# First loads of an encoder trunk on two queues, in smaller parts, and the first tile scaled ahead of the squares

## The chip, the cores and the metric

The kernel runs on one core of a Trainium2 chip. The metric is the device time of one execution, in microseconds (us). PE is the matmul engine, DVE and ACT are the vector and the scalar engine, POOL is GpSimd, and SP is the engine that issues most of the transfers; "SPq" and "ACTq" in the trace are transfers being issued on the queue of SP and of ACT.

## The reference

Two layers over 256 tokens of width 1024. Cut to what matters:

```python
for l in range(DEPTH):                       # DEPTH = 2
    h = rmsnorm(x, norm_g[l])
    proj = h @ w_in[l]                       # 1024 x 5120
    xa, za, qb, kb, vb, zb, qc, kc, vc, zc = jnp.split(proj, split_points, axis=-1)
    ya = ssm_branch(xa, ...) * jax.nn.silu(za)        # bidirectional state space group
    yb = na_branch(qb, kb, vb, na_rpb[l]) * jax.nn.silu(zb)
    yc = dilated_branch(qc, kc, vc, t5_bias) * jax.nn.silu(zc)
    x = x + jnp.concatenate([ya, yb, yc], axis=-1) @ w_out[l]
return rmsnorm(x, final_g)
```

The change lies in what comes first: x and the first weights are loaded, the squares of x give the RMS factor, and `h @ w_in[0]` begins.

## The kernel before, in words

All activations lie transposed: 128 partitions, 8 blocks k of the model width, 256 tokens. A layer multiplies h by w_in in 20 jobs c of 256 columns. A job has two weight pieces (k 0 to 3 and k 4 to 7), each `[4, 256]` per partition, 512 KB, in a buffer `raw`. Six jobs of layer 0 (0, 1, 2, 3, 5 and 8) are plain: PE reads the fp32 weights from `raw`. For the others ACT or DVE make a high part (`whi`) and DVE a low part (`wlo`), and PE does three matmuls for one. After the 20 jobs, among which the state space group and the heads are worked off, come the jobs of the output projection (`mix0`, `mix1`, `mix2`).

Jobs 0 and 1 of layer 0 don't wait for the RMS factor: they read `gx`, which is x times the gain `ng` (`scaled`, L1358: one 128x256 tile per k, on ACT or DVE), and the factor `rstd` is multiplied in afterwards, where DVE makes `xa`. From job 2 on PE reads `xin`, x with gain and `rstd` (`normed`, L1370, on DVE), and its split `h0h`, `h0l`, `h1h`, `h1l` (`split_h`, L1387). The way to `rstd`: ACT squares two k at a time (`sqx`), DVE adds the squares, PE sums over partitions (`psn<-ones,sqx`), ACT takes a root and DVE refines it (`nr`), PE spreads it (`psn<-ident,nr`), ACT copies it. In the same stretch DVE and ACT also make the state space group's tables (`sva`, `svb`, `lbar`, `pw`, `pt`, `q1`, `tmi`, `wt`); PE transposes `wt` in groups of four matmuls (`psw<-ident,wt`).

In the first microseconds `read_x` (L1528) issues on SP the gain, and then in turn a part of x (two k, 256 KB) and half of a weight piece (256 KB). The ACT queue carries one load only, the state space parameters `lam`. `load_pieces` (L474) follows on SP with the other pieces.

The order of the work on every engine is fixed when the program is built. Each piece of work is a generator that yields the engine it wants next and the events it waits for; a planner (`Flow`) keeps a clock for every engine from its own cost formulas, and emits what can start first, ranked by the tables `RANK` and `PATIENCE`. `in_order` then ties each engine to that order. Where the planner sees PE with nothing to do it puts in filler matmuls (`warm`, L438, called at L320 to L326), whose results nobody reads. All other instructions go through one helper and have line L135 in the trace, so tiles and not lines tell them apart.

Of the kernel before, what the change touches and what calls it, by code (L numbers as in the profile page):

```python
# [340 lines left out]
def trunk(ctx: ExitStack, tc: tile.TileContext, io):  # L341
# [18 lines left out]
    def dma(out, src):  # L360
        SP.dma_start(out, src)
# [25 lines left out]
    def events(n):  # L387
        return [Event() for _ in range(n)]
# [75 lines left out]
    class Piece:  # L464


        def __init__(self, src, plain=False):
            self.src, self.plain, self.by_dma = src, plain, False
            self.half_ev, self.raw_ev, self.hi_ev, self.ev = Event(), Event(), Event(), Event()

        def free(self):
            flow.free(*(("raw",) if self.plain else ("whi", "wlo")))
# [1 line left out]
    def load_pieces(pieces):  # L474
        for w in pieces:
            yield "SP", "raw"
            w.raw = new("raw", [4, 256])
            dma(w.raw, w.src)
            flow.set(w.half_ev)
            flow.set(w.raw_ev)  # L480
            if w.plain:
                flow.set(w.ev)
# [926 lines left out]
    def run_layer(L):  # L1409
# [3 lines left out]
        for kind, c, kgs in L.jobs:  # L1413
            if kind == "in":
# [4 lines left out]
                for kh in range(2):  # L1419
                    w = next(it)  # L1420
                    for kk in range(4):
                        yield "PE", w.half_ev if w.plain and kk < 2 else w.ev, (L.g_ev if early else L.h_ev if w.plain else L.hs_ev)[4 * kh + kk]
                        hx, h = (L.gx if early else L.hx)[kh], L.h[kh]
                        for ct in range(2):
                            first, last = kh == 0 and kk == 0 and ct == 0, kh == 1 and kk == 3
                            o = ps[:, ct * 256:(ct + 1) * 256]
                            cs = slice(ct * P, (ct + 1) * P)
                            if w.plain:
                                a, b = w.raw[:, kk, cs], hx[:, kk, :]
                                if toks:  # L1430
                                    a, b = hx[:, kk, cs], w.raw[:, kk, :]
                                mm(o, a, b, first, last)
                            elif toks:
                                mm3(o, [t[:, kk, cs] for t in h], [w.hi[:, kk, :], w.lo[:, kk, :]], first, last)
                            else:
                                mm3(o, [w.hi[:, kk, cs], w.lo[:, kk, cs]], [t[:, kk, :] for t in h], first, last)
                    w.free()
# [87 lines left out]
    LAST_PLAIN = [max(n, default=0) for n in PLAIN]  # L1525
    L0 = layers[0]

    def read_x():  # L1528

        yield "SP", "qkv", "qkv"  # L1530
        L0.hx = [new("qkv", [4, S], name=f"xin{i}") for i in range(2)]
        load_gain(L0)
        for i in range(4):
            dma(L0.hx[i // 2][:, 2 * (i % 2):2 * (i % 2) + 2, :], io["x"][:, 2 * i:2 * i + 2, :])
            flow.set(xin_ev[i])
            flow.cur.pend = 0.0

            w, k = pieces[i // 2], 2 * (i % 2)
            if k == 0:
                yield "SP", "raw"  # L1540
                w.raw = new("raw", [4, 256])
            else:
                yield "SP"
            dma(w.raw[:, k:k + 2, :], w.src[:, k:k + 2, :])
            flow.set(w.half_ev if k == 0 else w.raw_ev)
            if k:
                flow.set(w.ev)
            flow.cur.pend = 0.0
            yield "SP"
        flow.spawn(place_gx(L0))  # L1550
        yield "A", "atn"
        sq = new("atn", [8, S], name="sqx")
        done = events(4)
# [6 lines left out]

    def square_x(i, sq, ev, done):
        yield "A", ev
        flow.spawn(scaled(L0, 2 * i, 2))
        s = sq[:, 2 * i:2 * i + 2, :]
        A.activation(s, L0.hx[i // 2][:, 2 * (i % 2):2 * (i % 2) + 2, :], AF.Square)
        if i > 0:
# [12 lines left out]
        for ev in n.ev:  # L1579
            flow.set(ev)  # L1580

    begin, xin_ev = Event(), events(4)
    pieces = [w for L in layers for w in L.pieces]
    begin.t = 1.2
    flow.spawn(keep_warm(WARM[0], begin, L0.hs_ev[7]))
# [101 lines left out]
```

## Time and profile before

| | us |
|---|---|
| median of 3 runs | 459.48 (458.31 to 461.18) |
| profiled execution | 457.03 |
| its span in the trace | 455.2 |
| PE busy in the span | 444.5 |
| DVE busy | 349.6 |
| ACT busy | 301.5 |

The profiled execution is the one that the trace shows; its time contains the span and about 1.8 us around it. The mean granted clock of PE in it is 0.997. A row of a timeline gives the start, the length, the engine, the line, the operation, out<-in and the count; an fp32 matmul of 256 columns by fp32 weights leaves two records, so a count of 8 is four matmuls. Times in the text are those of the span's start unless said otherwise.

### The profile page before, as it was taken

What the parts mean: (1) busy time and instruction counts of PE and PEld (TensorE: products, weight loads), DVE (VectorE), ACT (ScalarE), POOL (GpSimd) and SP (SyncE); (2) the same over time, 40 slices, a digit from 0 to 9 for tenths busy, and PEclk for the clock granted to TensorE, in tenths of its full rate; (3) what the DMA queues carried; (4) which work ended last, traced back from release to release, by engine and by line L of the source; (5) the groups of instructions that cost most, each with busy time, mean ns of one, the idle gap of its engine ahead of it and who ended that gap; (6) DMA issues with size and microseconds to landing.
All of it is one profiled execution on the core that took longest, in us unless ns stands there. A gap on an engine that the chain in (4) does not pass through costs nothing.

```text
span 455.2 us, 11299 instructions
## 1 busy us (share of the span) xinstructions
PE 444.5 (98%) x4484; PEld 412.4 (91%) x4484; DVE 349.6 (77%) x747; ACT 301.5 (66%) x607; POOL 30.6 (7%) x61
## 2 busy tenths in 40 slices
PE   8999999998999999999999999999999999999994
PEld 7779899788888999999998999998998999999994
DVE  5899979998798688879728889499899654468533
ACT  6444889784687866846534687967787793756532
POOL 1020031210000000000000110232000000000000
PEclk9999999999999999999999999999999999999998
DMA  7755362545767344545626844755564654554503
GB/s 261 247 176 194 103 193 77 146 134 161 275 186 225 123 137 144 175 159 179 212 110 199 245 146 124 195 152 167 174 192 144 204 169 130 195 182 151 177 1 93
DMA packets 46005, 75.79 MB, mean 166 GB/s; under 512 B 20944, under 2 KB 29264, under 8 KB 45952
## 3 DMA queue, kind: packets, MB, share of 16 engines
q1 hardware_dynamic: 45808, 74.97, 52.3%
q8 instruction: 35, 0.57, 0.5%
q14 instruction: 18, 0.15, 0.1%
q10 hardware_dynamic: 144, 0.10, 0.1%
HBM read 70.38 MB, written 4.67 MB: 165 GB/s over the span
## 4 chain that ended last, share of the span: by engine, by line
PE 78%; DVE 9%; DMA 6%; ACT 3%; issue 1%; SPq 1%; POOL 0%; DVEq 0%; ACTq 0%; POOLq 0%
PE pj L135 58%; PE psy L135 4%; PE po L135 3%; PE sc L135 3%; PE psx L135 3%; PE pp L135 3%; DMA xad<-xa 2%; DMA raw<-w_in 2%; PE psn L135 2%; PE psw L135 2%; DMA xin<-x 1%; DMA bias<-rpb 1%; PE psr L135 1%; DVE t1s L135 1%; DVE wlo L135 1%
## 5 line engine op out<-in xcount | busy, mean ns | idle before, releaser
L135 DVE TENSOR_TENSOR wlo<-raw,whi 128x1024 fp32r<-128x1024 f32 x92 | 113.9, 1238 | 44.7 <-PE pj L135 25.5
L135 ACT CAST whi<-raw 128x1024 fp32r<-128x1024 f32 x92 | 96.1, 1046 | 63.1 <-PE pj L135 39.8
L135 PE MATMUL pj<-h0h,whi 128*128 128x256 f32 x192 | 57.2, 298 | 0.0
L135 PE MATMUL pj<-h1h,whi 128*128 128x256 f32 x192 | 56.2, 292 | 0.0
L135 PE MATMUL pj<-h0l,whi 128*128 128x256 f32 x192 | 54.3, 283 | 0.0
L135 PE MATMUL pj<-h1h,wlo 128*128 128x256 f32 x192 | 54.2, 283 | 0.0
L135 PE MATMUL pj<-h0h,wlo 128*128 128x256 f32 x192 | 54.2, 283 | 0.0
L135 PE MATMUL pj<-h1l,whi 128*128 128x256 f32 x192 | 54.2, 282 | 0.0
L135 POOL TENSOR_TENSOR bias<-bias,namask 128x160 f32<-128x160 f32 x32 | 25.6, 802 | 214.7 <-DMA bias<-rpb 177.3
L135 PEld LDWEIGHTS pj<-h0h,whi 128*128 128x128 f32 x192 | 36.7, 191 | 2.2 <-issue 1.9
L135 PEld LDWEIGHTS pj<-h1h,whi 128*128 128x128 f32 x192 | 36.7, 191 | 1.5 <-issue 1.2
L135 PEld LDWEIGHTS pj<-h0h,wlo 128*128 128x128 f32 x192 | 36.7, 191 | 0.1
L135 PEld LDWEIGHTS pj<-h1h,wlo 128*128 128x128 f32 x192 | 36.7, 191 | 0.0
L135 PEld LDWEIGHTS pj<-h1l,whi 128*128 128x128 f32 x192 | 36.7, 191 | 0.0
L135 PEld LDWEIGHTS pj<-h0l,whi 128*128 128x128 f32 x192 | 36.6, 191 | 0.0
L135 PE MATMUL pj<-xin,raw 128*128 128x256 f32 x128 | 31.4, 385 | 0.2 <-DVE xin L135 0.2
L135 ACT ACTIVATE pt<-pt,nm 128x160 f32<-128x160 f32 (+1 forms) x64 | 29.5, 463 | 0.8 <-DVE nm L135 0.7
L135 ACT ACTIVATE pt<-pt,sm 128x256 f32<-128x256 f32 (+1 forms) x62 | 26.9, 465 | 3.6 <-DVE sm L135 3.5
L135 PEld LDWEIGHTS pj<-xin,raw 128*128 128x128 f32 x128 | 22.9, 190 | 4.4 <-DVE xin L135 1.3
L135 ACT COPY E<-psx 64x512 f32<-64x512 f32 x32 | 18.6, 580 | 7.4 <-PE psx L135 6.9
L135 ACT COPY ptt<-pp 128x512 f32<-128x512 f32 x32 | 18.7, 585 | 6.8 <-PE pp L135 6.6
L135 PE MATMUL pj<-gx,raw 128*128 128x256 f32 x96 | 22.4, 384 | 0.0
(196 smaller groups left out, 1201.7 us busy)
## 6 DMA issues: line engine op xcount, KB each, us to landing
raw<-w_in SPq DMA_DIRECT2D x78, 512.0 KB, 3.7
raw<-w_out SPq DMA_DIRECT2D x24, 512.0 KB, 3.2
bias<-vdram SPq DMA_DIRECT2D x16, 192.0 KB, 3.4
raw<-glu_w SPq DMA_DIRECT2D x4, 512.0 KB, 3.1
bias<-rpb SPq DMA_DIRECT2D x16, 120.0 KB, 3.9
xin<-x SPq DMA_DIRECT2D x4, 256.0 KB, 5.2
raw<-w_in SPq DMA_DIRECT2D x4, 256.0 KB, 4.9
cc<-c_p SPq DMA_DIRECT2D x2, 512.0 KB, 6.4
```

The costliest lines, as they stand in the source:

```text
L135: return f(*args, **kw)
```

## The change

x goes out on SP in five parts (k 0, k 1, k 2-3, k 4-5, k 6-7). The two pieces of job 0 and the gain go out on the ACT queue (`read_w`), the first piece in parts k 0, k 1 and k 2-3, the second in two halves, each part with an event of its own on which PE waits. `half_ev` goes. Tiles of `gx` are asked for one by one, the one of k 0 before the squares.

```diff
--- before.py
+++ after.py
@@ -466,7 +466,7 @@
 
         def __init__(self, src, plain=False):
             self.src, self.plain, self.by_dma = src, plain, False
-            self.half_ev, self.raw_ev, self.hi_ev, self.ev = Event(), Event(), Event(), Event()
+            self.raw_ev, self.hi_ev, self.ev, self.part_ev = Event(), Event(), Event(), None
 
         def free(self):
             flow.free(*(("raw",) if self.plain else ("whi", "wlo")))
@@ -476,7 +476,6 @@
             yield "SP", "raw"
             w.raw = new("raw", [4, 256])
             dma(w.raw, w.src)
-            flow.set(w.half_ev)
             flow.set(w.raw_ev)
             if w.plain:
                 flow.set(w.ev)
@@ -1419,7 +1418,7 @@
                 for kh in range(2):
                     w = next(it)
                     for kk in range(4):
-                        yield "PE", w.half_ev if w.plain and kk < 2 else w.ev, (L.g_ev if early else L.h_ev if w.plain else L.hs_ev)[4 * kh + kk]
+                        yield "PE", w.part_ev[kk] if w.part_ev else w.ev, (L.g_ev if early else L.h_ev if w.plain else L.hs_ev)[4 * kh + kk]
                         hx, h = (L.gx if early else L.hx)[kh], L.h[kh]
                         for ct in range(2):
                             first, last = kh == 0 and kk == 0 and ct == 0, kh == 1 and kk == 3
@@ -1525,29 +1524,38 @@
     LAST_PLAIN = [max(n, default=0) for n in PLAIN]
     L0 = layers[0]
 
+    def read_w():
+
+        L0.ng = one("ng", [KD], bufs=2)
+        for n, w in enumerate(pieces[:2]):
+            w.part_ev = events(4)
+            for k, size in ((0, 1), (1, 1), (2, 2)) if n == 0 else ((0, 2), (2, 2)):
+                if k == 0:
+                    yield "A", "raw"
+                    w.raw = new("raw", [4, 256])
+                else:
+                    yield "A"
+                A.dma_start(w.raw[:, k:k + size, :], w.src[:, k:k + size, :])
+                for i in range(k, k + size):
+                    flow.set(w.part_ev[i])
+                flow.cur.pend = 0.0
+                if n == k == 0:
+                    A.dma_start(L0.ng, io["norm_g"][0])
+                    flow.set(L0.ng_ev)
+                    flow.cur.pend = 0.0
+
     def read_x():
 
         yield "SP", "qkv", "qkv"
         L0.hx = [new("qkv", [4, S], name=f"xin{i}") for i in range(2)]
-        load_gain(L0)
-        for i in range(4):
-            dma(L0.hx[i // 2][:, 2 * (i % 2):2 * (i % 2) + 2, :], io["x"][:, 2 * i:2 * i + 2, :])
-            flow.set(xin_ev[i])
-            flow.cur.pend = 0.0
-
-            w, k = pieces[i // 2], 2 * (i % 2)
-            if k == 0:
-                yield "SP", "raw"
-                w.raw = new("raw", [4, 256])
-            else:
-                yield "SP"
-            dma(w.raw[:, k:k + 2, :], w.src[:, k:k + 2, :])
-            flow.set(w.half_ev if k == 0 else w.raw_ev)
-            if k:
-                flow.set(w.ev)
+        flow.spawn(read_w())
+        for k, size in ((0, 1), (1, 1), (2, 2), (4, 2), (6, 2)):
+            dma(L0.hx[k // 4][:, k % 4:k % 4 + size, :], io["x"][:, k:k + size, :])
+            flow.set(x0_ev if k == 0 else xin_ev[k // 2])
             flow.cur.pend = 0.0
             yield "SP"
-        flow.spawn(place_gx(L0))
+        flow.spawn(place_gx(L0, x0_ev))
+        flow.spawn(scaled(L0, 0, 1))
         yield "A", "atn"
         sq = new("atn", [8, S], name="sqx")
         done = events(4)
@@ -1560,7 +1568,8 @@
 
     def square_x(i, sq, ev, done):
         yield "A", ev
-        flow.spawn(scaled(L0, 2 * i, 2))
+        for k in range(1 if i == 0 else 2 * i, 2 * i + 2):
+            flow.spawn(scaled(L0, k, 1))
         s = sq[:, 2 * i:2 * i + 2, :]
         A.activation(s, L0.hx[i // 2][:, 2 * (i % 2):2 * (i % 2) + 2, :], AF.Square)
         if i > 0:
@@ -1579,7 +1588,7 @@
         for ev in n.ev:
             flow.set(ev)
 
-    begin, xin_ev = Event(), events(4)
+    begin, x0_ev, xin_ev = Event(), Event(), events(4)
     pieces = [w for L in layers for w in L.pieces]
     begin.t = 1.2
     flow.spawn(keep_warm(WARM[0], begin, L0.hs_ev[7]))
```

Since a planner sets the order, it moves in places that the diff does not name. In the rows below `[waits ...]` names the counters that the instruction waits for: DMAHW0 to DMAHW7 are eight counters that the transfers of all queues use in turn, so a transfer that reuses one is issued after the earlier transfer on it has landed; the other names are engines.

ACT, from its first transfer on, before (raw is a weight piece, xin0 and xin1 are x, the numbers behind names tell buffers apart):

```order
L135 DMA svb_90<-lam 128x192
L135 ACTIVATE sqx_104<-xin0_84 128x512 [waits DMAHW1_49]
L135 ACTIVATE gx0_111<-xin0_84,ng_86 128x256 [waits DMAHW0_49]
L135 ACTIVATE gx0_111<-xin0_84,ng_86 128x256
L135 ACTIVATE sqx_104<-xin0_84 128x512 [waits DMAHW4_49]
L135 ACTIVATE gx0_111<-xin0_84,ng_86 128x256 x2
L135 ACTIVATE sqx_104<-xin1_85 128x512 [waits DMAHW6_49]
L135 ACTIVATE gx1_112<-xin1_85,ng_86 128x256 x2
L135 ACTIVATE sqx_104<-xin1_85 128x512 [waits DMAHW0_49]
L135 ACTIVATE gx1_112<-xin1_85,ng_86 128x256 x2
```

And ACT after the change:

```order
L135 DMA raw_89<-w_in 128x256
L135 DMA ng_86<-norm_g 128x8
L135 DMA svb_97<-lam 128x192
L135 DMA raw_89<-w_in 128x256 [waits DMAHW0_49]
L135 DMA raw_89<-w_in 128x512 [waits DMAHW2_49]
L135 DMA raw_107<-w_in 128x512 [waits DMAHW3_49]
L135 ACTIVATE sqx_101<-xin0_84 128x512 [waits DMAHW1_49]
L135 ACTIVATE gx0_105<-xin0_84,ng_86 128x256 [waits DMAHW5_49]
L135 ACTIVATE gx0_105<-xin0_84,ng_86 128x256
L135 DMA raw_107<-w_in 128x512 [waits DMAHW6_49]
L135 ACTIVATE sqx_101<-xin0_84 128x512
L135 ACTIVATE sqx_101<-xin1_85 128x512 [waits DMAHW4_49]
```

Between the loads of `lam` and the first square there now stand three transfers that wait for a landing: that of x k 0 (DMAHW0), of x k 2-3 (DMAHW2) and of the first part of the weights (DMAHW3); a fourth, before the second square, waits for x k 6-7 (DMAHW6). The first square still stands ahead of the first `gx`; on DVE the tiles k 2 and k 3 of `gx` are now its first work after two memsets.

PE at its start, after the change (before, 12 `warm`, 12 `gx` matmuls, and then the two of `psn<-ones,sqx`):

```order
L438 MATMUL warm_95<-ident_63 128x128 [waits Pool_49]
L438 MATMUL warm_95<-ident_63 128x128 x8
L135 MATMUL pj_92<-gx0_105,raw_89 128x256 [waits DMAHW3_49,Activation_49]
L135 MATMUL pj_92<-gx0_105,raw_89 128x256
L135 MATMUL pj_92<-gx0_105,raw_89 128x256 [waits DMAHW0_49,Activation_49]
L135 MATMUL pj_92<-gx0_105,raw_89 128x256
L438 MATMUL warm_95<-ident_63 128x128 x3
L135 MATMUL pj_92<-gx0_105,raw_89 128x256 [waits DMAHW2_49,DVE_49]
L135 MATMUL pj_92<-gx0_105,raw_89 128x256
L135 MATMUL psn_164<-ones_64,sqx_101 128x1 [waits DVE_49]
L135 MATMUL psn_164<-ones_64,sqx_101 128x1
L135 MATMUL pj_92<-gx0_105,raw_89 128x256 x2
```

The `psn<-ones,sqx` pair stands behind 6 matmuls of `gx`, and no longer behind 12. There are 9 `warm` ahead of the first and 3 between, where there were 12 ahead; the four that stood between the matmuls of job 2 are gone.

PE at the end of layer 0, where the `mix0` part of an output job ends, before:

```order
L135 MATMUL pj_2649<-mix0h_2175,wlo_2614 128x256
L135 MATMUL pj_2649<-mix0l_2176,whi_2561 128x256
L438 MATMUL warm_1982<-ident_63 128x128
L135 MATMUL pj_2649<-mix1h_2643,whi_2616 128x256 [waits Activation_49]
L135 MATMUL pj_2649<-mix1h_2643,wlo_2665 128x256 [waits DVE_49]
L135 MATMUL pj_2649<-mix1l_2644,whi_2616 128x256 [waits DVE_49]
```

And after the change:

```order
L135 MATMUL pj_2587<-mix0h_2203,wlo_2539 128x256
L135 MATMUL pj_2587<-mix0l_2204,whi_2503 128x256
L438 MATMUL warm_1935<-ident_63 128x128 x10
L135 MATMUL psw_2638<-ident_63,wt_2554 128x128 [waits DVE_49,Activation_49]
L135 MATMUL psw_2638<-ident_63,wt_2554 128x128 x3
L438 MATMUL warm_1935<-ident_63 128x128 x3
L135 MATMUL psw_2652<-ident_63,wt_2554 128x128 [waits DVE_49,Activation_49]
L135 MATMUL psw_2652<-ident_63,wt_2554 128x128 x3
L438 MATMUL warm_1935<-ident_63 128x128 x7
L135 MATMUL psw_2668<-ident_63,wt_2643 128x128 [waits DVE_49,Activation_49]
L135 MATMUL psw_2668<-ident_63,wt_2643 128x128 x3
L135 MATMUL pj_2587<-mix1h_2575,whi_2537 128x256
```

Twenty `warm` stand here instead of one, around three groups of `psw` of the next layer, which before stood among earlier jobs; a second single `warm` that followed 12 matmuls later is gone. In layer 1 both programs have the same order. In jobs 3 and 4 the change has two `psw` groups ahead of the first matmul of job 4, before it has four.

## Rows read from the trace of the kernel before

**Rows 1.** Page, engines: busy us (share of the span), instructions.

```profile
PE 444.5 (98%) x4484; PEld 412.4 (91%) x4484; DVE 349.6 (77%) x747; ACT 301.5 (66%) x607; POOL 30.6 (7%) x61
```

**Rows 2.** Timeline of SP's queue, 0 to 12: start us, us, engine, instruction, count.

```profile
1.19 0.42 SPq L135 DMA_DIRECT2D xin<-x  x1
2.12 0.45 SPq L135 DMA_DIRECT2D xin<-x  x1
...
7.00 0.56 SPq L135 DMA_DIRECT2D cc<-c_p  x1
```

**Rows 3.** Chain that ended last, 0 to 33: start us, us, what.

```profile
2.12 4.86 DMA xin<-x
```

**Rows 4.** Timeline of ACT, 0 to 33; in brackets idle time before and its releaser.

```profile
0.94 0.38 ACTq L135 DMA_DIRECT2D svb<-lam  x1
...
4.41 0.63 ACT L135 ACTIVATE sqx<-xin 128x512 f32<-128x512 f32 x1 [2.18 <-DMA xin<-x]
4.95 0.89 ACT L135 ACTIVATE gx<-xin,ng 128x256 f32<-128x256 f32 x2
...
14.11 0.26 ACT L135 ACTIVATE nr<-psn,epst 128x2 f32<-128x2 f32 x1
...
16.03 0.37 ACT L135 COPY rstd<-psn 128x256 f32<-128x256 f32 x1 [1.36 <-PE psn L135]
```

**Rows 5.** Timeline of DVE, 0 to 33.

```profile
4.53 1.01 DVE L135 SCALAR_TENSOR_TENSOR sva<-sva 128x64 f32<-128x64 f32 x4
7.66 0.69 DVE L135 TENSOR_TENSOR sqx<-sqx 128x512 f32<-128x512 f32 x1 [2.13 <-ACT sqx L135]
...
11.65 0.41 DVE L135 TENSOR_TENSOR sqx<-sqx 128x256 f32<-128x256 f32 x1
```

**Rows 6.** Timeline of PE, 0 to 42.

```profile
1.36 4.89 PE L438 MATMUL warm<-ident 128*128 128x128 f32 x24 [1.36 <-POOL ident masks.py:199]
6.16 5.64 PE L135 MATMUL pj<-gx,raw 128*128 128x256 f32 x24
12.12 0.60 PE L135 MATMUL psn<-ones,sqx 128*128 128x1 f32 x4 [0.31 <-DVE sqx L135]
...
15.28 0.71 PE L135 MATMUL psn<-ident,nr 128*128 128x128 f32 x4
...
23.02 2.16 PE L135 MATMUL pj<-xin,raw 128*128 128x256 f32 x8
...
27.69 0.61 PE L438 MATMUL warm<-ident 128*128 128x128 f32 x4
28.46 4.64 PE L135 MATMUL pj<-xin,raw 128*128 128x256 f32 x20 [0.16 <-DVE xin L135]
...
33.37 1.89 PE L135 MATMUL pj<-xin,raw 128*128 128x256 f32 x8
35.10 0.60 PE L135 MATMUL psw<-ident,wt 128*128 128x128 f32 x4
...
40.55 0.47 PE L135 MATMUL pj<-h0h,whi 128*128 128x256 f32 x1
```

**Rows 7.** Windows: us, busy time of each engine, PEclk, DMA share, GB/s.

```profile
8.00:10.00 2.00, 2.00 (x10) 1.71 (x10) 1.93 (x9) 2.00 (x6) 0.00 (x0) 1.00 1.03 344
...
20.00:40.00 20.00, 19.83 (x98) 16.43 (x98) 19.83 (x51) 7.30 (x19) 3.47 (x6) 1.00 0.61 189
```

**Rows 8.** PE's waits between 33 and 204: us in total, times, longest.

```profile
PE sc L135 <- ACT k L135: 1.3, 1, 1.3
PE pp L135 <- issue: 0.5, 1, 0.5
```

**Rows 9.** Timeline of PE at the end of layer 0.

```profile
209.96 0.39 PE L438 MATMUL warm<-ident 128*128 128x128 f32 x2
...
210.31 0.28 PE L135 MATMUL pj<-mix1h,wlo 128*128 128x256 f32 x1
210.42 0.29 PE L135 MATMUL pj<-mix1l,whi 128*128 128x256 f32 x1
```

## The prediction

> **What bounds the kernel now.** First the engines' line of the page [rows 1]: PE is busy for 444.5 us, 98% of the span of 455.2, in a fixed order. So a change pays only where PE idles or does filler, and costs wherever it puts either on PE. Then PE's timeline of the start [rows 6] shows where it isn't doing useful work: 4.89 us of filler from 1.36 to 6.16, the first real matmul at 6.16, and job 2 (`pj<-xin`), which begins at 23.02 but is fed by DVE with filler between, so that its second half and job 3 run only from 28.46. A plain matmul takes 1.73 / 4 = 0.43 us (8 records from 33.37 to 35.10), so the 16 of job 2 in one run would have ended at 29.9, and not at 28.46 + 8 x 0.43 = 31.9. Job 4 begins at 40.55. Behind the front, PE waits in layer 0 for 1.3 us (`sc<-k,q`) and for 0.5 us [rows 8].
>
> The other engines there: ACT squares x for 0.63 us a part and makes two tiles of `gx` in 0.89 [rows 4]; DVE adds squares, and between them works on `sva` at 0.25 us an instruction (4 in 1.01) [rows 5]; from 20 to 40 DVE is busy for 19.83 of 20 us [rows 7]. In the chain, x k 2-3, issued at 2.12, lands at 6.98 [rows 3]. The SP queue issues `cc` at 7.00, right behind that landing [rows 2]: an issue whose counter is still in use holds its queue until the earlier transfer is in.
>
> **The change, part by part.** All sums are against the profiled execution, 457.03 us, which is 2.45 us under the median of the runs shown.
>
> *Issues.* Three transfers leave SP (two weight halves of the first piece, the gain) and two more of the second piece; six come to ACT, at 0.38 us each by the one that stands there [rows 4] or 0.42 to 0.45 as on SP [rows 2]. The first three cost nothing, since ACT waits for x anyway until 4.41. The next three stand ahead of ACT's first square, and by the order each waits for a landing: x k 0, x k 2-3 and the first weight part. So x k 2-3 must be in before two issues, 0.85 us, and only then ACT begins to compute, though the square itself needs x k 0 and k 1 only. When does x k 2-3 land? At the earliest like the first x load of before, of as many bytes, 4.4 us [rows 4]; at the latest like the same part of before, 6.98. Ahead of it and with it are now about 740 KB against 870 KB before (sum of the loads issued by then on both queues); from 2 us on, where the first loads land, (6.98 - 2) x 740 / 870 gives 6.2 us as an estimate, and since it is issued half a microsecond earlier I take 6.0.
>
> *First tile.* 6.0 + 0.85 + the square (0.54, by the spacing 4.41 to 4.95) + a tile of `gx` (0.45, half of 0.89) gives the first real matmul at 7.9 us instead of 6.16. With the early bound it is 6.3. So the first tile isn't earlier in any case.
>
> *Squares and `rstd`.* Now ACT waits for x k 6-7 with a transfer before the second square: in by 8.4 us by the same scaling (bounds 6.5 and 9.6), plus 0.45, then square, square, two `gx`, square (3 x 0.54 + 0.8) to about 11.4, then DVE's two adds (0.69 and 0.41) to 12.5: `psn` at 12.5 against 12.12 [rows 6]. By then only 6 of 16 matmuls of job 0 are done, where before 12 were, because the order puts `psn` ahead of the others. Behind the last add DVE now has 11 instructions of `sva`, 11 x 0.25 = 2.7 us, ahead of its four of `nr`, which took 0.9 from ACT's end at 14.37 [rows 4] to PE's start at 15.28 [rows 6]: `psn<-ident,nr` at about 16.1. ACT's two lookups of `svb` stand ahead of `rstd` and wait for eight more `sva`, 2 us: `rstd` at about 18, not 16.03 [rows 4].
>
> *PE to job 4.* From 12.12 to 23.02 [rows 6] before has 10.9 us for 20 plain matmuls, 8.6, and 2.3 of other work. Now from 12.5: 26 matmuls x 0.43 = 11.2, the same 2.3, and 0.5 of wait, as `psn` (0.6) and 6 matmuls reach only to about 15.6: job 1 ends at 26.5, 3.5 us after 23.02. There the change gets something back: DVE and ACT now make `xin`, `h0` and `h1` ahead of the state space tables, so `xin` is there when PE comes. Job 2 takes 6.9 us instead of 9, and job 3 6.9 plus two `psw` groups of 0.45 (0.60 [rows 6] less the overlap with their neighbours). Job 4 starts at 26.5 + 6.9 + 6.9 + 0.9 = 41.2, 0.65 after 40.55 [rows 6], with two groups, 0.9 us, still to do: **+1.55 us**. If the landings come at the early bounds, 1.9 less for the last part of x: -0.4; if at the late ones, 1.2 more: +2.8.
>
> *Tables put off.* What DVE did from 16 to 23 us for the state space group comes after 26 us. DVE is full there [rows 7], so some of its products will be late for PE in jobs 4 and 5. A `wlo` that is late by a part of its own length: **+0.4 us** (0 to 1, where its slack is used up).
>
> *Later waits in layer 0.* A later PE swallows waits whose releasers aren't later too: from 1.8 us gone to as much again added. I take a gain of less than half: **-0.7 us** (-1.8 to +2).
>
> *Filler at the end of layer 0.* The order has 18 more `warm` there. Before, from the one `warm` at 209.96 to the second matmul after it 0.35 us pass, of which a matmul takes 0.11 to 0.12 [rows 9]: 0.23 each, 0.22 in a row of them (4 records in 0.61, with the end of the last [rows 6]). **+4.0 us**. They run whether or not PE has anything to wait for, and in before PE waits there for nothing at all [rows 8]. If DVE's late `wt` makes PE wait longer than the filler, it is more.
>
> Sum: 1.55 + 0.4 - 0.7 + 4.0 = **+5.25 us**, 462.3 in terms of the profiled execution, 464.7 of the median.
>
> **Row and rule, the first loads.** The transfers are busy at 1.03 of their engines' time from 8 to 10 us, at 344 GB/s [rows 7], fed by one queue nearly alone. The Trainium skill, "DMA: Bandwidth & Descriptors", section "Issuing engines are not separate DMA queues", says that transfers started on several engines end up on the same 16 and interleave, and that only issue time is saved. By that rule a second queue moves no byte earlier; the row agrees. It speaks against the early bounds above, which are already the less likely end.
>
> **The rivals.**
> *Nothing that can be measured.* The front is even, as the recovered 2 us of job 2 balance the later start, and the later waits shrink by 1.8: +4.0 + 0.4 - 1.8 = +2.6, 462.1 of the median, +0.6%. For it: job 2's starvation is large in the rows. Against: `rstd` is bound by DVE's `sva`. 0.35.
> *Faster.* Loads land at the early bounds, so the front gives back 1.9 + the whole of job 2's stall, about -4, and the moved tables let the waits of 1.8 go too. With the filler it is -1.8, 457.7. It decides at x k 6-7: in before 7.5 us. It can pass 1% (4.6 us) only if the filler isn't paid, that is if it takes the place of waits. 0.06 for all of it, 0.04 beyond 1%.
> *Slower still.* DVE, some 4 us behind at 30 us, doesn't catch up before the first whole `wlo` are due, and PE waits 3 to 4 us more in jobs 4 to 9: 468. For it: 19.83 of 20 us busy. Against: DVE is busy for 349.6 of 455.2 us in all [rows 1]. 0.13.
> *The clock.* In before, the first fillers take 4.89 / 12 = 0.41 us each [rows 6], later ones 0.22: PE begins at half pace, 1.2 GHz, and by the matmuls after 6.16 (24 records in 5.64, with waits on ACT) it is at 2.4. Now the 9 fillers end at about 5.2, and PE does nothing until 7.9. What it does at half pace before `psn` has room; if the first four matmuls behind `psn` still go at it, they cost 4 x 0.43 = 1.7 us more: 466.4. The longest idle time of PE after the start in before is 1.3 us [rows 8], so no row shows 2.7. 0.10. The Trainium skill, "TensorE: Matmul & The Clock Gate", section "Part 1: The HAM clock gate", says that activity releases a throttle and idleness brings it back, which is this rival; no run here shows it yet.
> *The change doesn't do what it says* is already in the forecast: the built order squares first.
>
> **How the numbers follow.** The forecast has 0.36, the four rivals 0.35, 0.06, 0.13 and 0.10. Likeliest time **464.7 us**. Eight in ten: from 459 (between the even and the faster case) to 469 (both slower mechanisms in part). A measurement of this kernel can tell about 1%, 4.6 us, from no change: 464.1 is the bound. The forecast lies at it, so half of its chance and all of the two slower rivals, with a tenth for sizes that I have too small, are slower: 0.50; faster 0.05; within 0.45.
>
> **What would show it.** Right: first real matmul between 6.3 and 8.7, `psn` at about 12.5, `rstd` after 17, job 2 in one run of about 7 us, job 4 between 40 and 42.5, and `warm` of 4 us at about 212 us with no idle time beside. Wrong: an ACT that squares at 4 us (then the transfers don't hold it), job 1 ending by 24, or fillers standing where PE would have waited anyway: then the `psw` behind them still shows a wait.

## The result and the profile after

The change makes the kernel slower: 466.50 us (465.96 to 467.94, four executions) against 460.33 (458.31 to 461.5, four) beside it. The ratio is 1.0144 [1.0096, 1.0191], or +6.2 us, against a forecast of 464.7 and +5.25. The profiled execution took 465.96 us with a span of 464.1, 8.9 more than that of before; 2.8 of these 8.9 arise behind the last `mix1` job, and are told apart below. Ratios leave out executions in a slower state of the clock; experiments 1 and 3 each have one among the four executions of their median, and the profile of experiment 3 is of it.

The page's line of engines answers to [rows 1] (busy us, share of the span, instructions):

```profile
PE 452.7 (98%) x4512; PEld 421.7 (91%) x4512; DVE 350.5 (76%) x748; ACT 299.2 (64%) x605; POOL 27.3 (6%) x61
```

PE is as full as before, and has only 28 records more. So the loss isn't idle time; it is PE's own work, which takes longer or is filler. The front shows the first kind. The chain that ended last, from 1.66 (start us, us, what):

```profile
1.66 4.33 DMA xin<-x
...
6.00 0.33 ACTq L135
...
6.38 0.45 ACTq L135
...
6.88 0.63 ACT sqx L135
```

ACT's timeline, answering to [rows 4]:

```profile
3.23 3.60 ACTq L135 DMA_DIRECT2D raw<-w_in  x3
...
17.78 0.37 ACT L135 COPY rstd<-psn 128x256 f32<-128x256 f32 x1 [0.86 <-PE psn L135]
```

The square at 6.88 needs x k 0 and k 1 only, yet stands behind three issues that last from 3.23 to 6.83, because the second of them waits for x k 2-3, in at 5.98. The last releaser that the view names is this landing; the two issues behind it (0.33 and 0.45) are the rest of the price. PE's timeline, to be laid beside [rows 6]:

```profile
1.35 4.21 PE L438 MATMUL warm<-ident 128*128 128x128 f32 x18 [1.35 <-POOL ident masks.py:199]
7.96 3.78 PE L135 MATMUL pj<-gx,raw 128*128 128x256 f32 x8 [2.40 <-ACT gx L135]
11.53 1.49 PE L438 MATMUL warm<-ident 128*128 128x128 f32 x6
12.81 1.45 PE L135 MATMUL pj<-gx,raw 128*128 128x256 f32 x4
14.10 0.50 PE L135 MATMUL psn<-ones,sqx 128*128 128x1 f32 x4
14.46 2.84 PE L135 MATMUL pj<-gx,raw 128*128 128x256 f32 x12
...
27.36 9.01 PE L135 MATMUL pj<-xin,raw 128*128 128x256 f32 x41
```

After 2.40 us without work the first four matmuls take (11.53 - 7.96) / 4 = 0.89 us each, twice the 0.43 of [rows 6]; the 12 records from 14.46 are at 0.45 again. The 9 fillers ahead of the gap ran at half pace too, 0.43 us apart up to the last, so in this execution PE had not come to full pace when its work ran out. `psn` could have run when DVE's last add ended at 11.90, and came at 14.10. From 27.36 on job 2 runs without a gap, and job 3 up to a wait of 0.99 us for `wt` ahead of the `psw` at 40.60. DVE's timeline (the counterpart of [rows 5]):

```profile
6.00 0.62 DVE L135 TENSOR_SCALAR gx<-xin,ng 128x256 f32<-128x256 f32 x2 [5.11 <-DMA xin<-x]
...
11.48 0.42 DVE L135 TENSOR_TENSOR sqx<-sqx 128x256 f32<-128x256 f32 x1
...
28.84 0.29 DVE L135 TENSOR_TENSOR lbar<-svb,sva 128x128 f32<-128x128 f32 x1
```

In before `lbar` was there at 14.10:

```profile
14.10 0.29 DVE L135 TENSOR_TENSOR lbar<-svb,sva 128x128 f32<-128x128 f32 x1
```

So DVE idles for 5.11 us for x k 2-3, which its first tile of `gx` needs, with the tables' work queued behind. `lam`, which that work reads, was itself in only at about 6.2 (issued at 1.84, 4.4 us to its landing), so with another order on DVE the tables, which began at 6.54, would not have begun much earlier. The sum rows of two sets of windows, 0 to 14 and 14 to 40, say how much it lost (sum of us, then each engine's busy time). Before:

```profile
sum 14.00, PE 12.33 PEld 10.83 DVE 8.61 ACT 9.87 POOL 1.38; mean PE 2.06 PEld 1.80 DVE 1.43 ACT 1.64 POOL 0.23
sum 26.00, PE 25.83 PEld 20.83 DVE 24.89 ACT 9.99 POOL 3.47; mean PE 6.46 PEld 5.21 DVE 6.22 ACT 2.50 POOL 0.87
```

After:

```profile
sum 14.00, PE 10.25 PEld 8.99 DVE 5.88 ACT 6.07 POOL 1.38; mean PE 1.71 PEld 1.50 DVE 0.98 ACT 1.01 POOL 0.23
sum 26.00, PE 25.61 PEld 21.33 DVE 21.68 ACT 9.72 POOL 2.48; mean PE 6.40 PEld 5.33 DVE 5.42 ACT 2.43 POOL 0.62
```

By 40 us DVE has done 27.6 us of work instead of 33.5, though in all it does the same [rows 1]: 5.9 us are still to do. Of these 2.7 are lost by 14 us and 3.2 later, where DVE waits 3.6 us instead of 0.6, 1.67 of it for the transfer of `xa`. The work between doesn't make up for it: by 190 us DVE has done 154.2 us instead of 162.9. The lag shows at the end of layer 0, where DVE makes layer 1's `wt`. PE's matmuls on it before, and then after (duration in ns, first and last start in us):

```profile
L135 PE MATMUL psw<-ident,wt x32: 271/272/273, 165.0 to 185.7; 128*128 128x128 f32 x32
```

```profile
L135 PE MATMUL psw<-ident,wt x32: 270/273/273, 186.8 to 208.4; 128*128 128x128 f32 x32
```

They stand 22 us later, six of the eight groups past the start of `mix0`, and fillers stand ahead of three of them. PE's timeline after, where before has one `warm`, at 192.24 (that of [rows 9] is another one, 17.7 us later, which after has too, at 216.44):

```profile
192.01 2.40 PE L438 MATMUL warm<-ident 128*128 128x128 f32 x20
194.25 0.60 PE L135 MATMUL psw<-ident,wt 128*128 128x128 f32 x4
194.68 0.83 PE L438 MATMUL warm<-ident 128*128 128x128 f32 x6
195.35 0.60 PE L135 MATMUL psw<-ident,wt 128*128 128x128 f32 x4
195.79 1.73 PE L438 MATMUL warm<-ident 128*128 128x128 f32 x14
197.35 0.60 PE L135 MATMUL psw<-ident,wt 128*128 128x128 f32 x4
197.71 0.36 PE L135 MATMUL pj<-mix1h,whi 128*128 128x256 f32 x1
```

PE's longest waits between 33 and 204, answering to [rows 8] (us in total, times, longest):

```profile
PE psw L135 <- DVE wt L135: 1.0, 1, 1.0
PE pp L135 <- POOL bias L135: 0.7, 1, 0.7
```

The first places where each job begins give the account. A group of `psw` that is still to do counts 0.43 us (194.25 to 194.68):

| PE's first matmul of | before | after | later by | groups of `psw` still to do, more than before | lag |
|---|---|---|---|---|---|
| job 4 | 40.55 | 43.17 | 2.62 | 2 | 3.5 |
| `mix0` | 189.36 | 189.06 | -0.30 | 6 | 2.3 |
| `mix1` | 192.38 | 197.71 | 5.33 | 3 | 6.6 |
| `mix2` | 213.20 | 219.68 | 6.48 | 0 | 6.5 |
| last `mix1`, layer 1 | 436.46 | 442.55 | 6.09 | 0 | 6.1 |
| last matmul | 449.43 | 458.71 | 9.28 | 0 | 9.3 |

So 3.5 us are lost in the front, and 1.2 come back in the jobs: 0.9 of it as waits, which were 1.8 in [rows 8] and are now 0.7 and one of 0.2 (the wait for `wt` of 1.0 lies ahead of job 4). Between `mix0` and `mix1` 4.3 are added, which is 19 fillers of 0.23. From the last `mix1` to the last matmul 3.2 more are lost, and that is the clock. Windows of after (us, busy time of each engine, PEclk, DMA share, GB/s):

```profile
440.00:450.00 10.00, 10.00 (x89) 10.00 (x88) 2.84 (x4) 2.81 (x7) 0.00 (x0) 1.00 0.01 2
450.00:451.00 1.00, 1.00 (x10) 1.00 (x9) 0.00 (x0) 0.97 (x3) 0.00 (x0) 0.78 0.00 0
...
453.00:459.00 6.00, 6.00 (x29) 5.84 (x28) 2.35 (x7) 1.37 (x4) 0.00 (x0) 0.50 0.30 87
```

The granted clock falls to the 1.2 GHz level at about 450.5 with PE busy throughout, and a matmul that took 0.11 us takes 0.21. The profiled execution of before has 1.00 up to PE's end:

```profile
448.00:452.00 4.00, 1.57 (x11) 1.19 (x10) 2.26 (x7) 0.38 (x2) 0.00 (x0) 1.00 0.59 171
```

Executions of before differ in this too: those at a mean clock of 0.997 or 0.998 took 456.6 to 457.7 us, the others, from 0.975 to 0.994, took 457.5 to 465.1. The profiled one is 3.3 us under its median here, while that of after is 0.5 under its own; this is why the profiles differ by more than the medians. All four executions of after lay at 0.977 to 0.985. The loads don't decide it alone: experiments 1 and 6, which have the change's loads, take 12.97 us from the last `mix1` to the last matmul, like before, and experiment 8, which has not, takes 17.17. Whether the change has a part in it stays open.

### The profile page after: what moved, and what is told of

The parts are those of the page before. It is cut to its first block, busy times and chain, and to the rows that moved or that the text cites. A ratio compares the mean times of both kernels' runs of the same rounds, so it can differ in the third digit from the quotient of the medians.

```text
span 464.1 us, 11356 instructions
## 1 busy us (share of the span) xinstructions
PE 452.7 (98%) x4512; PEld 421.7 (91%) x4512; DVE 350.5 (76%) x748; ACT 299.2 (64%) x605; POOL 27.3 (6%) x61
## 4 chain that ended last, share of the span: by engine, by line
PE 82%; DMA 7%; DVE 5%; ACT 3%; issue 1%; SPq 0%; POOL 0%; ACTq 0%; DVEq 0%; POOLq 0%
PE pj L135 60%; PE psy L135 4%; PE po L135 4%; DMA xad<-xa 3%; PE pp L135 3%; PE sc L135 3%; PE warm L438 2%; PE psx L135 2%; PE psn L135 2%; PE psw L135 2%; DMA bias<-rpb 1%; DMA raw<-w_in 1%; DMA xin<-x 1%; PE psr L135 1%; DVE xa L135 1%; ACT whi L135 1%
## 5 line engine op out<-in xcount | busy, mean ns | idle before, releaser
L135 ACT CAST whi<-raw 128x1024 fp32r<-128x1024 f32 x91 | 95.1, 1048 | 55.2 <-PE pj L135 33.6
L135 POOL TENSOR_TENSOR bias<-bias,namask 128x160 f32<-128x160 f32 x32 | 22.1, 691 | 208.8 <-DMA gb<-glu_b 90.0
L135 ACT ACTIVATE pt<-pt,sm 128x256 f32<-128x256 f32 (+1 forms) x63 | 28.0, 465 | 5.1 <-DVE sm L135 4.9
L135 PE MATMUL pj<-xin,raw 128*128 128x256 f32 x128 | 29.9, 383 | 0.0
L135 PE MATMUL pj<-gx,raw 128*128 128x256 f32 x96 | 24.6, 410 | 2.4 <-ACT gx L135 2.4
L135 PEld LDWEIGHTS pj<-gx,raw 128*128 128x128 f32 x96 | 19.1, 206 | 6.1 <-ACT gx L135 2.7
```

Source lines behind the costliest of these rows:

```text
L135: return f(*args, **kw)
```

## The experiments

Two theories stood against each other from the start. **Clock and filler**: the front is lost to PE's half pace, and the fillers cost what they last. **Late DVE**: the tables that DVE begins late make layer 1's `wt` late, and the fillers only cover a wait that would be there anyway. The times of a job's start are from one profiled execution each, and such a time carries only so far: in experiment 10, the kernel before once more, job 4 began at 41.72 and `mix2` at 215.69, 1.2 and 2.5 us after the table's. The ratios are against runs of the kernel before on the same chip. Fillers in the edits are `flow.idle()`.

**1. The fillers at the end of layer 0 left out** (after, with 22 fillers that emit nothing, 20 of them there):

```diff
+        flow.idle = (lambda: None) if dry else lambda: nc.tensor.matmul(...)
-    flow.spawn(keep_warm(WARM[1], L0.sc_ev, layers[1].hs_ev[7]))
+    flow.spawn(keep_warm(WARM[1], L0.sc_ev, layers[1].hs_ev[7], dry=True))
```

> The changed kernel with the order as it is, without the 24 filler matmuls from the last heads of layer 0 to the middle of layer 1 (20 of them stand at the end of layer 0). Theory A (the fillers are what costs there, as the prediction had it: 0.22 us each): 4 to 5 us faster than the change, about 462, and mix1 begins 3.5 to 4.5 us after the last mix0 matmul less than now. Theory B (DVE's wt comes late, at 193.97 and 196.98 in the trace of the change, and the fillers only cover a wait that PE would have anyway): within 1 us of the change, 466, and PE's waits show 3 to 4.5 us of psw <- DVE wt in place of the fillers; mix1 still begins at about 197.5.

467.65 us, ratio 1.0171 [1.009, 1.0252]. PE's timeline there:

```profile
190.44 0.63 PE L135 MATMUL psw<-ident,wt 128*128 128x128 f32 x4 [0.21 <-DVE wt L135]
192.18 0.63 PE L135 MATMUL psw<-ident,wt 128*128 128x128 f32 x4 [1.11 <-DVE wt L135]
194.59 0.63 PE L135 MATMUL psw<-ident,wt 128*128 128x128 f32 x4 [1.78 <-DVE wt L135]
```

`mix0` to `mix1` takes 7.85 us where it took 8.65. Of 4.3 us of filler 0.8 are won; 3.1 turn into idle time that ends with DVE's `wt`. The fillers take the place of a wait. The 0.8 don't last either: behind the idle time the granted clock is at 0.50 from 195.4 to 198.8, and `mix1` to `mix2` takes 23.54 us instead of 21.97.

The front of this run has the order of after, and yet job 4 begins at 41.56 instead of 43.17:

```profile
8.15 3.42 PE L135 MATMUL pj<-gx,raw 128*128 128x256 f32 x8 [3.15 <-ACT gx L135]
11.41 0.83 PE L438 MATMUL warm<-ident 128*128 128x128 f32 x6
```

Here the fillers ahead of the gap came to full pace (0.22 us from 4.28 on), the row of the granted clock reads 0.50 from 7.7 to 11.0, and the fillers at 11.41 are at full pace, where those at 11.53 of after are not. How long the half pace lasts differs from one execution of the same front to the next.

**2. Twelve more fillers ahead of the first matmul** (after):

```diff
+                        if l == c == kh == kk == 0:
+                            for _ in range(12):
+                                flow.idle()
```

> The changed kernel with 12 more filler matmuls ahead of the first matmul of job 0, so that PE isn't idle from 5.3 to 7.96; nothing else moves. Theory A (the idle 2.4 us keep PE at half pace, and that holds psn until 14.1): the first matmuls take 0.43 and not 0.86 each, psn at about 12.1 as DVE's sums are ready at 11.9, job 4 at about 41.2 and not 43.17; the total 1 to 2 us less than the change. Theory B (the late loads and ACT's queue hold the front, and the pace of PE is hidden): psn before 13 all the same, job 4 at 43, total as the change.

465.29 us, 1.0164 [1.0121, 1.0206]. PE's start:

```profile
1.36 6.33 PE L438 MATMUL warm<-ident 128*128 128x128 f32 x42 [1.36 <-POOL ident masks.py:199]
7.92 1.99 PE L135 MATMUL pj<-gx,raw 128*128 128x256 f32 x8 [0.24 <-ACT gx L135]
...
12.16 0.50 PE L135 MATMUL psn<-ones,sqx 128*128 128x1 f32 x4
```

The first matmul comes no earlier, yet the four take 1.84 us instead of 3.57, and `psn` stands at 12.16, job 4 at 40.45, 2.7 before that of after. At `mix2` it still leads by 2.4. That is the clock's share in the profiled execution of after, shown by giving PE idle work; against experiment 1, whose front is that of after, it is 1.1 at job 4. In the median it is 1.2 of 466.5, and by the ratios (1.0164 against 1.0144) nothing: less than the intervals can tell. `mix2` remains 4.1 later than in before.

**3. The four weight loads behind the first issued by SP** (after; the planner's charges as they were, so the order too):

```diff
-                A.dma_start(w.raw[:, k:k + size, :], w.src[:, k:k + size, :])
+                if n == k == 0:
+                    A.dma_start(w.raw[:, k:k + size, :], w.src[:, k:k + size, :])
+                else:
+                    part = (w.raw[:, k:k + size, :], w.src[:, k:k + size, :])
+                    flow.charge("A", "dma_start", part, {})
+                    nc.sync.dma_start(*part)
```

> The changed kernel with the four weight loads after the first moved from the queue of ACT to that of SP; the order of all computing stays. Theory A (ACT is held by issues that wait for landings): ACT's first square at 4 to 4.5 and not 6.88, first real matmul at 5.3 to 6 and not 7.96, PE hardly idle before it and so at full pace from then on, job 4 at 40 to 41.5; 2 to 3 us less than the change. Theory B (the first parts land late in any case, and on SP the weights come behind all of x): the first square at 4.4, but PE waits 2 us or more for the second part of the weights, and job 4 begins at 42.5 to 43.5, total as the change.

464.44 us, 1.012 [1.0059, 1.0181]. ACT squares at 5.00 instead of 6.88, PE's first matmul starts at 6.08, so the issues did hold ACT. But the weights now stand behind x:

```profile
7.77 1.10 PE L135 MATMUL pj<-gx,raw 128*128 128x256 f32 x4 [0.56 <-DMA raw<-w_in]
...
11.24 1.10 PE L135 MATMUL pj<-gx,raw 128*128 128x256 f32 x4 [1.70 <-DVE sva L135]
...
12.64 3.55 PE L135 MATMUL pj<-gx,raw 128*128 128x256 f32 x8
```

PE idles for 1.70 us ahead of 11.24, and behind it the pace halves (8 records in 3.55). The releaser named there, `sva`, is only DVE's newest work: the `gx` that PE needs was made at 5.96 to 6.57. By the times it waited for the third part of the weights, issued by SP at 5.96: the loads of `raw` take up to 5.4 us from issue to landing, which gives 11.3 or so. Job 4 starts at 42.85, 0.3 before that of after. The Trainium skill, "TensorE: Matmul & The Clock Gate", section "Part 1: The HAM clock gate", has idleness bring the throttle back. This run agrees, with 1.70 us of idle time ahead of the matmuls at half pace, and so do the 3.15 us of experiment 1; the 0.24 us of experiment 2 had matmuls at full pace behind them. The 2.40 us of after say nothing on it, since PE was at half pace ahead of them already.

**4. The loads alone, without the first tile's part** (after):

```diff
-        flow.spawn(scaled(L0, 0, 1))
-        for k in range(1 if i == 0 else 2 * i, 2 * i + 2):
-            flow.spawn(scaled(L0, k, 1))
+        flow.spawn(scaled(L0, 2 * i, 2))
```

> The loads of the change (two queues, smaller parts) without the part on the first tile: tiles are asked for two by two by the squares, as before. In the built order the start of ACT and PE is that of the change, but at the end of layer 0 there are 2 fillers as before and no psw groups between mix0 and mix1. Theory A (what costs at the end of layer 0 is an order that the first-tile part sets off): front as the change, job 4 at 43.2; from mix0 to mix1 3.0 us and not 8.65; total 462 to 464. Theory B (the loads alone make DVE late to the end of the layer): the same order waits for wt elsewhere, and the total is as the change, 466.

468.81 us, 1.0243 [1.0184, 1.0303]. `mix0` to `mix1` takes 3.02 us, as in before, and yet `mix2` comes at 221.67, later than in after. The time went elsewhere:

```profile
PE pj L135 <- DVE wlo L135: 3.0, 1, 3.0
```

The wait ends at 45.74, in job 4: in this order the scan goes on, and the weight halves of a job are late instead. Behind the wait PE is busy at the lower clock for 10 us, which costs some 5 us more (half of 10.10):

```profile
45.60:55.70 10.10, 9.96 (x60) 9.62 (x61) 7.34 (x13) 3.37 (x5) 0.00 (x0) 0.50 0.31 105
```

So the loss is there with the loads alone and without the first tile's part, and the place where it shows is the planner's choice.

**5 and 6. `lam` first again** (after, with `lam` issued ahead of the weights on ACT; 5 has the edit of experiment 3 too):

```diff
+        flow.set(lam_go)          # beside the load of lam
-                    yield "A", "raw"
+                    yield "A", "raw", lam_go
```

> The changed kernel with lam issued first on ACT's queue and the four later weight loads on SP's, so ACT waits for no landing and DVE can begin the state space tables at about 2.9 as before, and not at 6.5; the planner answers with another order (tables ahead of xin on DVE as before, psw of the next layer spread over the last jobs, 15 fillers ahead of mix1). Theory A (what costs behind the front is DVE's work at the start, some 3 us lost while it waits for x): job 4 at 40 to 41, mix2 at 212 to 215, total like before, 457 to 461. Theory B (small parts and the planner's answer to them cost by themselves): mix2 at 217 or later, total 463 to 466.

> The changed kernel with lam issued first on ACT's queue, the weight loads still on it; computing in the same order as the run with the loads on SP, so the pair shows what the held ACT costs alone. ACT's first square at 6.9 and first real matmul at about 8 (one more issue stands ahead of gx), PE idle for 2 us and at half pace after. Theory A (held ACT and half pace together are the cost of the front): job 4 2 to 3 us later than in the run with the loads on SP, of which 1.5 to 3 remain at mix2. Theory B (DVE bounds the front): job 4 within 1 us of it.

465.17 us, 1.0121 [1.0036, 1.0206], and 467.94, 1.0177 [1.0108, 1.0246]. The tables are early again (`lbar` at 14.8 and 16.2), but `mix2` comes at 218.24 and 219.18, with 15 fillers ahead of `psw` in both. Job 4 starts at 47.48 and 48.45; this order has two groups of `psx`, 2.0 us each, ahead of it, so its start doesn't compare. By the count of the table, the lag of experiment 5 is 2.1 at `mix0` (190.62, two groups of `psw` still to do) and 5.0 at `mix2`. So the late `lam` alone isn't it either: with early tables layer 1's `wt` is still late in this order. Between the two runs, ACT's issues and PE's pace behind them make 0.97 at job 4.

**7. Before, with six needless adds on DVE**, 3.6 us by the plan, behind `xin` k 7:

```diff
+            if L.l == 0 and k == 7:
+                junk = one("junk", [512])
+                for _ in range(6):
+                    nc.vector.tensor_add(junk, ones.to_broadcast([P, 512]), ones.to_broadcast([P, 512]))
```

> The kernel before with six dummy adds of 128x512 on DVE, 3.6 us, ahead of the last h1l of layer 0: the order and all else as before. Theory A (DVE has no slack that PE doesn't need in layer 0, so what DVE loses at the start comes back as waits of PE): 2 to 3.6 us slower than before, first seen at job 4 to 6. Theory B (DVE's slack later takes it in): mix0 of layer 0 within 0.7 us of before, total within 1 us.

463.8 us, 1.0105 [1.0038, 1.0172]. The adds take DVE from 30.98 to 35.72, which is 4.7 us. PE waits at once:

```profile
PE psw L135 <- DVE wt L135: 3.4, 1, 3.4
```

Job 4 comes 5.5 later, at 46.06: to the wait is added a granted clock of 0.50 behind it, from 38.0 to 41.4. At `mix0` and `mix2` 3.62 are left against the profile of before, and 1.13 against that of experiment 10. So DVE time lost in the front comes back as a wait of PE. The work between doesn't absorb all of it, as the ratio says too; how much it absorbs isn't shown.

**8. Before, with only the tables held back** until x k 4-5 is in (loads as before):

```diff
-        yield "V"
+        yield "V", xin_ev[2]      # ahead of the first operation on lam
```

> The kernel before, its loads and its front as they are, but the state space tables wait for the third part of x (8.3 us) and not for lam alone (2.8 us). The planner answers as it did to the change: DVE makes xin ahead of the tables, and at the end of layer 0 five groups of psw of the next layer stand between mix0 and mix1, with 36 fillers. Theory A (the state space work that starts late on DVE, and so comes late at every step to the end of the layer, is what costs; not the loads): first matmul at 6.2 and full pace as before, yet mix2 at 218 to 221 and 5 to 8 us slower than before. Theory B (the loads and PE's pace cost, the order at the end of the layer doesn't): mix2 at 213 to 215, total within 2 us of before.

466.45 us, 1.011 [1.0047, 1.0173]. The first matmul comes at 6.55 and at full pace, job 2 runs in one piece, and job 4 starts at 37.76, 2.8 *ahead* of before, or 1.1 when the four groups of `psw` still to do are counted. And then, between `mix0` (184.11) and `mix1` (197.13):

```profile
186.99 3.73 PE L438 MATMUL warm<-ident 128*128 128x128 f32 x32
...
197.13 0.36 PE L135 MATMUL pj<-mix1h,whi 128*128 128x256 f32 x1
```

`mix2` comes 5.8 later than in before. No load was moved. The planner's answer is like that to the change: DVE makes tiles of `gx` first and idles 5.63 us for x. The late tables, with the order that the planner gives them, are enough for the loss, at the same place and with 36 fillers instead of 20.

**9. Experiment 3 with fillers between the first matmuls** (15 of them):

```diff
+                        if l == c == kh == 0:
+                            for _ in range((4, 3, 8, 0)[kk]):
+                                flow.idle()
```

> The changed kernel with the four later weight loads on SP's queue and 15 fillers in the gaps of the first six matmuls, so that PE stays at full pace; order else as the change. Theory A (the held ACT costs only by way of PE's pace, as the weights then come behind x): psn at about 12.2, job 4 at 40 to 40.8, like the run with 12 fillers and ACT held (40.45). Theory B (the held ACT costs by itself): psn at 10 to 11 and job 4 at 38.5 to 39.5. By both mix2 at 217 to 218, as the tables are late in both.

463.34 us, 1.0055 [1.0015, 1.0094], the best ratio of those with the change's loads, and still slower. `psn` at 13.04 and job 4 at 42.09 missed both forecasts, since the fillers were too many: PE works on them up to the third pair of matmuls at 12.17, which in experiment 3 could start at 11.24.

```profile
9.71 2.62 PE L438 MATMUL warm<-ident 128*128 128x128 f32 x22
```

`mix2` stands at 218.4, 5.2 after before's.

**10. Before once more**, for the clock.

> The kernel before once more, for its clock: executions of it came at a mean granted clock of 0.997 and of 0.986. If the trace has the lower one, it lies in the last 13 us, as in the change, and the last matmuls take 0.21 and not 0.11.

461.36 us, span 459.6, mean clock 0.990: the expectation on the tail missed. The tail was at full clock; the low stretches were 250 to 300, and this one (us, busy time of each engine, PEclk, DMA share, GB/s):

```profile
100.00:150.00 50.00, 48.11 (x512) 43.25 (x516) 42.89 (x112) 34.22 (x81) 0.00 (x0) 0.97 0.60 192
```

So before's executions lose clock at more than one place, and a single profiled execution can't say how much of a tail is the kernel's. By this row 1.5 us (0.03 of 50) of the 2.5 by which `mix2` stands later here are the clock's.

**11 and 12. The scan of layer 0 ranked otherwise in the planner**, with experiment 9 and with experiment 8:

```diff
-            ... ssm_scan=-0.012, ...
+            ... ssm_scan=(0.3, -0.012), ...
```

> The changed kernel with the weights on SP's queue, 15 fillers in the front and, in the planner's table, more patience for the scan of the state space group in layer 0 (0.3 for -0.012): psw of the next layer then stands among the jobs ahead of the output projection and no fillers remain between mix0 and mix1. Theory A (the change's price is the late state space work): mix0 to mix1 3 us, mix2 at 212 to 215 and not 218.4, total 457 to 461, about 4 us under the same kernel without it. Theory B (moving it only moves the wait): mix2 at 217 or later, total 462 to 465.

> The kernel before with the late tables of the earlier run (job 4 at 37.8, 2.8 us ahead of before, but mix2 at 219) and the same patience for the scan. Theory A: the front's gain stays and the end of the layer costs nothing more, so mix2 at 210 to 214 and the total 1 to 4 us under the kernel before. Theory B: DVE's work is the same and PE waits for it elsewhere, mix2 at 215 or later, total as before or slower.

478.53 us, 1.0375 [1.0331, 1.0419], and 475.95, 1.0326 [1.0276, 1.0377]. `mix0` to `mix1` is 2.9 us in both, as wished, but DVE then owes a `wlo` to a job of the first projection. Experiment 11 is slower than either theory had it; experiment 12 goes as theory B. The wait in experiment 11 (in 12 it is 15.7):

```profile
PE pj L135 <- DVE wlo L135: 16.1, 1, 16.1
```

No version tried beats the kernel before.

## Why the prediction was right, and where not

The time, 466.50, lies in the range and on the side named likeliest. In part that is luck, as the terms show.

*ACT held by issues: right.* x k 2-3 was in at 5.98 (6.0 said), the square came at 6.88 (6.85), the first matmul at 7.96 (7.9). Experiment 3 takes the issues away and has the square at 5.00.

*`psn` at 12.5: wrong in this execution.* It came at 14.10, because PE was at half pace, which was the rival given 0.10. Its price was put at 1.7 us; experiment 2 gives 2.7 at job 4 and 2.4 at `mix2`, and the front of experiment 1, the same order, 1.1 at job 4, with `psn` at 12.94. `nr` on PE at 17.14 instead of 16.1 follows from it.

*`rstd` after 17: met by luck.* It came at 17.78 (18 said), but ACT had waited 0.86 us for PE's `psn` then, which was late by the pace. In experiment 2, where DVE's `sva` and ACT's lookups come last ahead of it, as the prediction had it, it came at 16.25.

*Job 4 and the front: the term was mis-sized.* 41.2 and +1.55 were said, 43.17 and +3.5 measured, with two groups still to do in both. At full pace it is 40.45 (experiment 2), so the rest of the front was priced 0.75 too high and the clock, which the sum left to a rival, made 2.7. Job 2 in one run: right.

*Later waits: right in sign.* The wait of 1.3 us (`sc<-k,q`) is gone, and waits shrink by 0.9 in all (0.7 said).

*Tables put off, +0.4 by a `wlo` in jobs 4 and 5: the step that failed.* No `wlo` waits there (in the order of experiment 4 one does, for 3.0 us). The tables return as a late `wt` at the end of the layer, and they are the larger part of the loss: by the profile of before 4.1 us with the clock's share taken away (experiment 2), and 5.8 with no load moved (experiment 8). The second profile of before is 2.5 later at `mix2`, so the sizes are rough; that there is a loss is shown by the ratio of experiment 8 too.

*Fillers at the end of layer 0, +4.0: the size is right (4.3), the place and the reason wrong.* They were said to stand at about 212 us, by the `warm` of [rows 9], and stand at 192 to 197.4. "They run whether or not PE has anything to wait for" counts them as a cost of their own. Experiment 1 shows 3.1 us of wait under them; they were a sign of the late DVE that the planner saw. That before has no wait there was no argument, since in before `psw` was long done. Nor was the sign that the prediction named for this case, a `psw` behind the fillers that still waits: there is none in after, because the fillers cover the wait in full. So two terms were in each other's place, and the sum came out near only as the planner had priced the wait in fillers.

*Rivals.* "Faster" needed x k 6-7 before 7.5. ACT's issue that waits for it went out at 7.66, so it was in by then, earlier than the 8.4 of the sum and close to that point, but PE's pace had taken the time already. "Slower still" had the right engine and the wrong place. The tail's clock, 2.8 of the 8.9 of the profiled executions, was in no rival; before's executions lose clock too, the one of experiment 10 at other places.

What is open: DVE's deficit at 40 us and the lag at `mix2` don't map one to one (5.9 and 6.5 in after; 33.5 - 30.4 = 3.1 and 4.1 in experiment 2; 33.5 - 30.0 = 3.5 and 5.8 in experiment 8; 33.5 - 31.9 = 1.6 and 5.0 in experiment 5, with early tables). How much each order of the planner adds to the bare deficit wasn't taken apart. So a rival stands: that almost any change of what the planner is given leads it to an order that is worse by some us. Only experiment 7, which keeps the order, speaks for the deficit by itself.

## What to carry to other kernels

A transfer that must wait for a landing belongs on a queue whose engine has nothing to compute behind it, though in experiment 3 this won only 0.3 us at job 4, as the weights then came behind x. Where two engines are nearly full, cost a change by the busy time that the second one has lost in the front, and follow the order to where that work is next due; a filler in the new order was here a wait that the planner foresaw, and is to be priced as the wait. With an order that a planner has made for one set of arrival times, an edit that speeds up one arrival can lose more than it wins, and turning the planner's numbers afterwards moved the wait here and removed none.

## What the hardware showed that was not expected

- PE at half pace up to about 13.7 us in after, through its first fillers, 2.40 us without work and the first matmuls, while the row of the granted clock reads 1.00 from the start. In experiment 1 the same row reads 0.50 from 7.7 to 11.0, but 1.00 for the fillers at half pace up to 4.1: at the start of a trace the durations tell the pace, and the clock's row only in part.
- The clock at its 1.2 GHz level in the last 8 us of after with PE busy for 6.00 of 6.00 us; the stretch from the last `mix1` to the end takes 16.16 us instead of 12.97. Idle time doesn't explain this one.
- A long wait of PE cost twice here. In experiment 12 PE waits 15.71 us for a `wlo`, up to 129.38, and what follows runs at the lower level for 5.9 us, with PE busy throughout:

```profile
129.40:135.30 5.90, 5.90 (x25) 4.86 (x25) 5.83 (x17) 3.80 (x12) 0.00 (x0) 0.50 0.72 235
```

- A small transfer behind large ones on a second queue isn't early. The load of `lam` (KB, median us from issue to landing), before and then after; issued first on its queue again, it took 2.8 and 2.5 in experiments 5 and 6:

```profile
svb<-lam ACTq DMA_DIRECT2D x1, 96.0 KB, 1.9
```

```profile
svb<-lam ACTq DMA_DIRECT2D x1, 96.0 KB, 4.4
```

The Trainium skill, "DMA: Bandwidth & Descriptors", section "Issuing engines are not separate DMA queues", says that transfers from several engines share the same engines and interleave; the 4.4 us agree.
